# Retention: scores of two heads in turn, rotation and norm two steps ahead of the products that read them

## The chip, the cores and the metric

One core of a Trainium2 chip runs the whole kernel as one program. The metric is the device time of one execution in microseconds (us), the median of several runs.

## What is computed

The reference is a decoder of two layers over 1024 positions of width 1024. In each layer four mixers (softmax attention with forget gates, a gated linear recurrence, RWKV-7 and retention) each take 256 of the width, then come an output projection, cross attention and an MLP, each with norms around it. The change touches retention alone, with four heads of 64 and chunks of 128 positions:

```
qh = rotary(q); kh = rotary(k) / 8                    # per head, 64 wide
inner = einsum('bhcnd,bhcmd->bhcnm', qc, kc) * dmat   # scores in a chunk, decay mask
intra = einsum('bhcnm,bhcme->bhcne', inner, vc)
kv    = einsum('bhcmd,bhcme->bhcde', kc * zeta, vc)
R_next = R * chunk_decay + kv                         # state, chunk after chunk
cross = einsum('bhcnd,cbhde->bhcne', qc * xi, R)
o = head_rms_norm(intra + cross, w)                   # o * rsqrt(mean(o*o) + eps) * w, per head
return o * silu(g)
```

## The kernel before

One generator writes each branch of the mixer stage: the dense projections, RWKV in four quarters, the recurrence, the forget-gate attention (called fox), the keys and values of the memory, and retention (`ret`, from L943). A generator stops at each `yield`; one step of it is what stands between two of them. The function `weave` in `run`'s layer goes round: one step of each RWKV chain, one step of retention, then three or four pieces of `fill`, which are the dense products, fox and, at the end, the first products of the output projection. Retention begins with the last RWKV quarter. That quarter has 16 rounds, so 16 retention steps; after it `weave` runs retention alone with the fill, two of its steps and four fill pieces a round. The program is then built by a planner that orders each engine's queue by the written order and by when it expects operands and buffers to be ready, so that work written later can stand earlier in a queue. On the chip each queue runs in the order that it has.

A tile of retention is 128 positions, eight tiles a layer. Before the change it goes through four steps:

- `rotate` (L962): two loads on SP's queue (L964, L965), four VectorE instructions of the rotation (L970 to L974), the decayed keys (L976), the gate (L977 on ScalarE, L978), then four TensorE transposes into one PSUM bank (L981) and its two readers, a copy on ScalarE (L983) and a product on VectorE (L985).
- `retain`, first step: for each head of a pair two score products of 64 rows into one bank (L996), then the mask on VectorE (L997).
- `retain`, second step: the output products (L1001, L1004), the state products (L1010), the state update on VectorE (L1014), two readers of the output on ScalarE (L1016, L1017).
- `finish` (L1020): sum of squares (L1026), the power on GpSimd (L255, L256 in `rstd`), two multiplies on VectorE (L1028, L1029), two transposes into one bank (L1032), each followed by its scaled copy on ScalarE (L1033), and after every fourth tile two stores.

The loop (L1041) writes, in each pass, the rotation of tile tt, both steps of tile tt-1 and the finish of tile tt-2. All PSUM banks of retention, and those of the RWKV chain, are of the tag "r", which has two; a bank is waited for as a whole. The SBUF tiles of retention, RWKV and fox's weights are of one tag of 32 buffers (`q`, L487). A matmul on these float32 operands shows in the trace as two instructions.

Of the kernel before, what the change touches and what calls it, by code (L numbers as in the profile page):

```python
# [11 lines left out]
ALU = mybir.AluOpType  # L12
AX = mybir.AxisListType
# [9 lines left out]
EPS = 1e-6  # L23
GN_EPS = 64e-5
NT = S // 128
# [61 lines left out]
class Kern:  # L87
# [855 lines left out]
    def ret(self, l, tmq, tmv, mixd):  # L943
        nc = self.nc
        V, A, P, T = nc.vector, nc.scalar, nc.gpsimd, nc.tensor
        H = lambda shape=(128, 512), name="re": self.q(shape, name)
        tab = [H((128, 4, 2, 2, 32), name="rot") for _ in range(2)]
        for i in range(2):
            self.dma2(tab[i].rearrange("p a b c d -> p (a b c d)"), self.I["rot"][:, 512 * i:512 * i + 512])
        dm = H((128, 4, 128), name="rdm")  # L950
        self.dma2(dm.rearrange("p h n -> p (h n)"), self.I["retc"][:, 0:512])
        rc = H((128, 512), name="rec")
        self.dma2(rc[:, 0:256], self.I["retc"][:, 512:768])
        xi, Rb = (rc[:, 256 * i:256 * i + 256].rearrange("p (a n) -> p a n", a=2) for i in range(2))
        rz = self.small([128, 6], "rtz", 1)
        self.dma2(rz, self.I["retc"][:, 768:774])
        zeta, dec = rz[:, 0:4], rz[:, 4:6]
        V.memset(Rb, 0.0)
        hd = lambda ap: ap.rearrange("p (h d) -> p h d", h=4)
        out = {}  # L960

        def rotate(tt):  # L962
            x, vg, xc, xs = H(), H(), H(), H()
            self.dma2(x, tmq[tt])  # L964
            self.dma2(vg, tmv[tt])  # L965
            g = vg[:, 256:512]
            q8 = lambda ap: ap.rearrange("p (q h d) -> p q h d", q=2, h=8)
            cb = tab[tt // 4][:, tt % 4, :, 0, :].unsqueeze(2).to_broadcast([128, 2, 8, 32])
            sb = tab[tt // 4][:, tt % 4, :, 1, :].unsqueeze(2).to_broadcast([128, 2, 8, 32])
            V.tensor_tensor(q8(xc), q8(x), cb, ALU.mult)  # L970
            V.tensor_tensor(q8(xs), q8(x), sb, ALU.mult)
            g4 = lambda ap: ap.rearrange("p (g e d) -> p g e d", g=8, e=2)
            V.tensor_tensor(g4(x)[:, :, 0], g4(xc)[:, :, 0], g4(xs)[:, :, 1], ALU.subtract)
            V.tensor_tensor(g4(x)[:, :, 1], g4(xs)[:, :, 0], g4(xc)[:, :, 1], ALU.add)  # L974
            kz, sg = xc[:, 0:256], xc[:, 256:512]
            V.tensor_tensor(hd(kz), hd(x[:, 256:512]), zeta.unsqueeze(2).to_broadcast([128, 4, 64]), ALU.mult)  # L976
            A.activation(sg, g, AF.Tanh, scale=0.5)  # L977
            V.scalar_tensor_tensor(sg, sg, 1.0, g, ALU.add, ALU.mult)  # L978
            pt = self.psum("r", (128, 4, 128))
            for j in range(4):  # L980
                T.transpose(pt[:, j], x[:, 128 * j:128 * j + 128], self.ident)  # L981
            qk = H((128, 4, 128))
            A.copy(qk, pt)  # L983
            qx = xs[:, 0:256].rearrange("p (a n) -> p a n", a=2)
            V.tensor_tensor(qx, pt[:, 0:2], xi, ALU.mult)  # L985
            return x, vg, xc, xs, qk

        def retain(tt, x, vg, xc, xs, qk):
            v, kz = vg[:, 0:256], xc[:, 0:256]
            qx = xs[:, 0:256].rearrange("p (a n) -> p a n", a=2)  # L990
            inn = x.rearrange("p (a n) -> p a n", a=4)
            for h in range(2):
                pi = self.psum("r", (128, 2, 128))
                rs = slice(64 * h, 64 * h + 64)
                for ct in range(2):
                    T.matmul(pi[:, ct], qk[rs, 2 + ct], qk[rs, ct], start=True, stop=True)  # L996
                V.tensor_tensor(inn[:, h:4:2], pi, dm[:, h:4:2], ALU.mult)  # L997
            yield
            po = self.psum("r", (128, 256))
            for ct in range(2):  # L1000
                T.matmul(po[:, 128 * ct:128 * ct + 128], qx[:, ct], Rb[:, ct], start=True, stop=False)  # L1001
                for h in range(2):
                    c0 = 128 * ct + 64 * h
                    T.matmul(po[:, c0:c0 + 64], inn[:, 2 * ct + h], v[:, c0:c0 + 64], start=False, stop=h == 1)  # L1004
            if tt < NT - 1:
                pk = self.psum("r", (128, 2, 64))
                for ct in range(2):
                    for h in range(2):
                        c0 = 128 * ct + 64 * h
                        T.matmul(pk[64 * h:64 * h + 64, ct], kz[:, c0:c0 + 64], v[:, c0:c0 + 64], start=True, stop=True)  # L1010
                for ct in range(2):
                    for h in range(2):
                        rs = slice(64 * h, 64 * h + 64)
                        V.scalar_tensor_tensor(Rb[rs, ct, rs], Rb[rs, ct, rs], dec[rs, ct:ct + 1], pk[rs, ct],  # L1014
                                               ALU.mult, ALU.add)
            A.copy(xs[:, 256:512], po)  # L1016
            A.activation(xs[:, 0:256], po, AF.Square, scale=0.125)  # L1017
            yield

        def finish(tt, x, vg, xc, xs, qk):  # L1020
            if tt % 4 == 0:
                out[0] = [H((128, 512), name="ost") for _ in range(2)]
            ost = out[0]
            y, sg = xs[:, 256:512], xc[:, 256:512]
            ss = self.small([128, 4], "ress", 2)
            V.tensor_reduce(ss, hd(xs[:, 0:256]), AX.X, ALU.add)  # L1026
            r = self.rstd(ss, EPS, 4, "t")
            V.tensor_tensor(hd(y), hd(y), r.unsqueeze(2).to_broadcast([128, 4, 64]), ALU.mult)  # L1028
            V.tensor_tensor(y, y, sg, ALU.mult)  # L1029
            py = self.psum("r", (128, 2, 128))  # L1030
            for ct in range(2):
                T.transpose(py[:, ct], y[:, 128 * ct:128 * ct + 128], self.ident)  # L1032
                A.activation(ost[ct][:, (tt % 4) * 128:(tt % 4) * 128 + 128], py[:, ct], AF.Copy,  # L1033
                             scale=self.half(l, "ret_w", ct))
            if tt % 4 == 3:
                t0 = 512 * (tt // 4)
                for ct in range(2):
                    self.dma2(mixd[3][ct][:, t0:t0 + 512], ost[ct])

        st = {}  # L1040
        for tt in range(NT + 2):  # L1041
            if tt < NT:
                st[tt] = rotate(tt)
                yield
            if 0 <= tt - 1 < NT:
                yield from retain(tt - 1, *st[tt - 1])
            if tt >= 2:
                finish(tt - 2, *st.pop(tt - 2))
                yield


    def fox_gates(self, l, vfd, cd):
# [731 lines left out]
    def layer(self, l, hT, vfirst, first, pj):  # L1784
# [71 lines left out]

        tm = [0, 0]
        retg = ret()
        kv = [self.dram([128, 4, 256], "kd") for _ in range(2)], [self.dram([128, D], "vd") for _ in range(2)]
        x = self.xd[3 * l:3 * l + 4]  # L1860
# [160 lines left out]
```

## Time and profile before

| | |
|---|---|
| median of 3 runs | 3272.2 us (3271.38 to 3275.03) |
| the profiled execution | 3271.57 us, its span 3269.8 us |
| TensorE (PE) busy | 3116.0 us, 95% of the span |
| VectorE (DVE) | 2098.6 us, 64% |
| ScalarE (ACT) | 1307.2 us, 40% |
| GpSimd (POOL) | 804.6 us, 25% |
| mean granted TensorE clock | 0.978 of full speed |
| retention, layer 0 and layer 1 | from about 455 to 612 us and 2090 to 2242 us |

Matmuls are pipelined and their ends are modelled, so that the busy time of PE is not its rate: how far apart two instructions start tells more. A wait is shown with what released it. The clock is given as a part of full speed.

### The profile page before, as it was taken

Reading aid. Unit: us, or ns where it says so; the run is one execution under the profiler, and the core shown is the slowest. Engines: PE = TensorE matmul, PEld = TensorE weight load, DVE = VectorE, ACT = ScalarE, POOL = GpSimd, SP = SyncE. Lnnn points to the kernel's source line nnn. Section 1 sums busy time; section 2 is a strip of 40 time slices with the busy share of each in tenths; the row PEclk is TensorE's granted clock in tenths of the full one; section 3 lists DMA queues with packets and bytes.
Section 4 is the critical chain, followed back from the end, with each engine's and each line's share of the span. In section 5 each row is a group of like instructions: output and inputs, shape, how many; then the busy total and the mean of one; then the engine's idle time right before and its main releaser. Section 6 shows DMA issues by size and latency. Waiting matters only on the chain. (4 is left out here: it accounts for less than half of the span.)

```text
span 3269.8 us, 47116 instructions
## 1 busy us (share of the span) xinstructions
PE 3116.0 (95%) x17888; PEld 2526.2 (77%) x17888; DVE 2098.6 (64%) x3424; ACT 1307.2 (40%) x2396; POOL 804.6 (25%) x654
## 2 busy tenths in 40 slices
PE   8999999999998999899999999999999889999998
PEld 6777777878876888788777677778788768878886
DVE  4566567364457766888835765673644666668896
ACT  5345444343433222533433454443444432235332
POOL 1000121010014786333000001210100148853330
PEclk9999999999998999999999999999999999999999
DMA  5322363252333445544433234632523334455433
GB/s 176 103 85 91 112 201 110 75 189 73 110 110 107 157 152 183 176 164 138 140 131 111 97 88 116 201 94 97 168 78 97 116 114 152 154 176 196 156 132 125
DMA packets 220995, 429.31 MB, mean 131 GB/s; under 512 B 51136, under 2 KB 98368, under 8 KB 220768
## 3 DMA queue, kind: packets, MB, share of 16 engines
q1 hardware_dynamic: 214112, 409.32, 37.7%
q0 software_dynamic: 6656, 16.98, 2.1%
q8 instruction: 141, 2.31, 0.3%
q14 instruction: 86, 0.70, 0.1%
HBM read 294.51 MB, written 131.69 MB: 130 GB/s over the span
## 5 line engine op out<-in xcount | busy, mean ns | idle before, releaser
L212 PE MATMUL p<-hT,wl 128*128 128x512 f32 x1536 | 605.0, 395 | 17.2 <-DVE wl L198 17.0
L210 PE MATMUL p<-hT,wh 128*128 128x512 f32 x1536 | 615.7, 401 | 4.7 <-ACT mc L1526 2.5
L211 PE MATMUL p<-hT,wh 128*128 128x512 f32 x1536 | 605.1, 394 | 0.0
L198 DVE TENSOR_TENSOR wl<-wraw,wh 128x1024 fp32r<-128x1024 f32 (+1 forms) x230 | 281.2, 1223 | 346.6 <-ACT wh L197 345.9
L197 ACT CAST wh<-wraw 128x1024 fp32r<-128x1024 f32 (+1 forms) x230 | 240.0, 1044 | 487.7 <-POOL wraw L1472 182.4
L246 PE MATMUL p<-bo,ao 128*128 128x512 f32 x912 | 358.0, 393 | 15.7 <-DVE mb L1544 15.7
L248 PE MATMUL p<-bo,ao 128*128 128x512 f32 x912 | 357.2, 392 | 3.9 <-DVE bo L198 3.9
L247 PE MATMUL p<-bo,ao 128*128 128x512 f32 x912 | 357.4, 392 | 0.0
L212 PEld LDWEIGHTS p<-hT,wl 128*128 128x128 f32 x1536 | 291.8, 190 | 84.1 <-DVE wl L198 22.3
L210 PEld LDWEIGHTS p<-hT,wh 128*128 128x128 f32 x1536 | 292.1, 190 | 79.1 <-issue 13.2
L211 PEld LDWEIGHTS p<-hT,wh 128*128 128x128 f32 x1536 | 292.2, 190 | 57.5 <-issue 0.7
L246 PEld LDWEIGHTS p<-bo,ao 128*128 128x128 f32 x912 | 172.7, 189 | 52.6 <-DVE mb L1544 16.6
L246 PE MATMUL p<-wh,mt 128*128 128x512 f32 x512 | 204.6, 400 | 2.6 <-ACT wh L197 1.5
L248 PEld LDWEIGHTS p<-bo,ao 128*128 128x128 f32 x912 | 172.7, 189 | 40.8 <-DVE bo L198 4.7
L256 POOL TENSOR_TENSOR rs<-ssq,neghalf 128x1 f32<-128x1 f32 x48 | 26.1, 543 | 719.9 <-DVE ssq L303 533.1
L248 PE MATMUL p<-wl,mt 128*128 128x512 f32 x512 | 201.8, 395 | 0.6 <-DVE wl L198 0.5
L247 PE MATMUL p<-wh,mt 128*128 128x512 f32 x512 | 201.6, 394 | 0.0
L247 PEld LDWEIGHTS p<-bo,ao 128*128 128x128 f32 x912 | 172.6, 189 | 35.7
L198 DVE TENSOR_TENSOR ao<-araw,ao 128x1024 fp32r<-128x1024 f32 x106 | 173.2, 1634 | 14.1 <-ACT ao L197 14.0
L198 DVE TENSOR_TENSOR bo<-braw,bo 128x1024 fp32r<-128x1024 f32 x92 | 146.8, 1600 | 44.7 <-ACT bo L197 44.7
L197 ACT CAST bo<-braw 128x1024 fp32r<-128x1024 f32 x92 | 96.6, 1052 | 186.1 <-PE p L247 124.7
L197 ACT CAST ao<-araw 128x1024 fp32r<-128x1024 f32 x106 | 111.5, 1052 | 107.5 <-DMA araw<-hd 91.3
(393 smaller groups left out, 6303.8 us busy)
## 6 DMA issues: line engine op xcount, KB each, us to landing
araw<-hd SPq DMA_DIRECT2D x106, 512.0 KB, 4.0
x<-x SPq DMA_DIRECT2D x80, 512.0 KB, 3.5
wraw<-in_mlp_w SPq DMA_DIRECT2D x68, 512.0 KB, 3.5
braw<-in_mlp_w SPq DMA_DIRECT2D x64, 512.0 KB, 4.7
wraw<-in_w_fm SPq DMA_DIRECT2D x32, 512.0 KB, 3.8
pj<-spl SPq DMA_DIRECT2D x64, 256.0 KB, 2.1
hd<-mb SPq DMA_DIRECT2D x64, 256.0 KB, 2.5
hd<-mc SPq DMA_DIRECT2D x64, 256.0 KB, 2.0
```

What stands on the lines that cost most here:

```text
L197: self.nc.scalar.copy(h, src)
L198: self.nc.vector.tensor_tensor(lo, src, h, ALU.subtract)
L210: mm(ps, wh, xl, start=first, stop=False)
L211: mm(ps, wh, xh, start=False, stop=False)
L212: mm(ps, wl, xh, start=False, stop=last)
L246: mm(ps, xl, wh, start=first, stop=False)
L247: mm(ps, xh, wh, start=False, stop=False)
L248: mm(ps, xh, wl, start=False, stop=last)
L256: P.tensor_tensor(r, ss, self.neghalf[:, 0:k], ALU.pow)
```

## The change

In the new code `rotate` ends with the gate, and its transposes and their readers are a function of their own, `turned`. The scores are a function `scores`, which takes both banks first and issues the products of the two heads in turn, then both masks. The norm (`norm`) is split from `finish`, with the multiply by the gate moved ahead of the one that needs the power; `finish` issues both transposes and then both copies. The loop writes, for a tile: scores of tt and rotation of tt+1; then finish of tt-1 and the output and state of tt; then the transposes of tt+1; then the norm of tt. There are 37 steps a layer in place of 32.

```diff
+        def turned(x, vg, xc, xs):
             pt = self.psum("r", (128, 4, 128))
             for j in range(4):
                 T.transpose(pt[:, j], x[:, 128 * j:128 * j + 128], self.ident)
             qk = H((128, 4, 128))
             A.copy(qk, pt)
-            qx = xs[:, 0:256].rearrange("p (a n) -> p a n", a=2)
-            V.tensor_tensor(qx, pt[:, 0:2], xi, ALU.mult)
-            return x, vg, xc, xs, qk
+            V.tensor_tensor(xs[:, 0:256].rearrange("p (a n) -> p a n", a=2), pt[:, 0:2], xi, ALU.mult)
+            return qk
+
+        def scores(x, vg, xc, xs, qk):
+            inn = x.rearrange("p (a n) -> p a n", a=4)
+            pi = [self.psum("r", (128, 2, 128)) for _ in range(2)]
+            for ct in range(2):
+                for h in range(2):
+                    rs = slice(64 * h, 64 * h + 64)
+                    T.matmul(pi[h][:, ct], qk[rs, 2 + ct], qk[rs, ct], start=True, stop=True)
+            for h in range(2):
+                V.tensor_tensor(inn[:, h:4:2], pi[h], dm[:, h:4:2], ALU.mult)
...
         def retain(tt, x, vg, xc, xs, qk):
-            for h in range(2):
-                pi = self.psum("r", (128, 2, 128))
-                rs = slice(64 * h, 64 * h + 64)
-                for ct in range(2):
-                    T.matmul(pi[:, ct], qk[rs, 2 + ct], qk[rs, ct], start=True, stop=True)
-                V.tensor_tensor(inn[:, h:4:2], pi, dm[:, h:4:2], ALU.mult)
-            yield
...
-            yield
-
-        def finish(tt, x, vg, xc, xs, qk):
...
+        def norm(x, vg, xc, xs, qk):
             y, sg = xs[:, 256:512], xc[:, 256:512]
             ss = self.small([128, 4], "ress", 2)
             V.tensor_reduce(ss, hd(xs[:, 0:256]), AX.X, ALU.add)
             r = self.rstd(ss, EPS, 4, "t")
+            V.tensor_tensor(y, y, sg, ALU.mult)
             V.tensor_tensor(hd(y), hd(y), r.unsqueeze(2).to_broadcast([128, 4, 64]), ALU.mult)
-            V.tensor_tensor(y, y, sg, ALU.mult)
+
+        def finish(tt, x, vg, xc, xs, qk):
...
             for ct in range(2):
                 T.transpose(py[:, ct], y[:, 128 * ct:128 * ct + 128], self.ident)
+            for ct in range(2):
                 A.activation(ost[ct][:, (tt % 4) * 128:(tt % 4) * 128 + 128], py[:, ct], AF.Copy,
                              scale=self.half(l, "ret_w", ct))
...
-        st = {}
-        for tt in range(NT + 2):
-            if tt < NT:
-                st[tt] = rotate(tt)
-                yield
-            if 0 <= tt - 1 < NT:
-                yield from retain(tt - 1, *st[tt - 1])
-            if tt >= 2:
-                finish(tt - 2, *st.pop(tt - 2))
-                yield
+        st = {0: rotate(0)}
+        yield
+        yield
+        st[0].append(turned(*st[0]))
+        yield
+        for tt in range(NT):
+            scores(*st[tt])
+            if tt + 1 < NT:
+                st[tt + 1] = rotate(tt + 1)
+            yield
+            if tt:
+                finish(tt - 1, *st.pop(tt - 1))
+            retain(tt, *st[tt])
+            yield
+            if tt + 1 < NT:
+                st[tt + 1].append(turned(*st[tt + 1]))
+            yield
+            norm(*st[tt])
+            yield
+        yield
+        finish(NT - 1, *st.pop(NT - 1))
+        yield
```

## Rows read from the trace of the kernel before

**Rows 1.** Windows: busy us (instructions) of PE, PEld, DVE, ACT, POOL; clock, DMA, GB/s.

```profile
455.00:612.00 157.00, 147.30 (x1203) 118.07 (x1202) 110.08 (x253) 68.81 (x138) 25.18 (x37) 0.93 0.38 118
...
2090.00:2242.00 152.00, 142.27 (x1137) 115.06 (x1136) 108.77 (x261) 64.01 (x133) 21.18 (x31) 0.89 0.35 108
```

**Rows 2.** Waits of PE, whole run: total us, times, longest.

```profile
PE p L981 <- DVE re L974: 7.5, 4, 2.3
...
PE p L1032 <- DVE re L1029: 1.5, 2, 0.8
PE p L1032 <- ACT ost L1033: 1.3, 2, 0.9
```

**Rows 3.** Timeline of PE: start, us, line, tiles, count [idle before, releaser].

```profile
569.14 1.12 PE L981 MATMUL p<-ident,re 128*128 128x128 f32 x4 [2.08 <-DVE re L974]
...
2188.15 0.66 PE L981 MATMUL p<-ident,re 128*128 128x128 f32 x4 [1.32 <-DVE re L974]
...
2195.77 0.33 PE L1032 MATMUL p<-ident,re 128*128 128x128 f32 x1 [0.88 <-ACT ost L1033]
2197.83 1.12 PE L981 MATMUL p<-ident,re 128*128 128x128 f32 x4 [1.74 <-DVE re L974]
```

**Rows 4.** Windows of 10 us at the end of both retention stages.

```profile
560.00:570.00 10.00, 7.36 (x54) 6.00 (x53) 6.92 (x14) 5.28 (x11) 3.48 (x7) 0.94 1.06 274
570.00:580.00 10.00, 10.00 (x41) 7.89 (x40) 7.61 (x18) 3.22 (x7) 2.77 (x5) 0.50 0.34 89
580.00:590.00 10.00, 10.00 (x46) 7.70 (x44) 4.88 (x12) 4.30 (x10) 1.17 (x2) 0.88 0.26 86
...
2190.00:2200.00 10.00, 7.39 (x46) 5.27 (x44) 8.32 (x18) 4.56 (x11) 5.47 (x8) 0.85 0.70 218
2200.00:2210.00 10.00, 9.98 (x50) 9.30 (x49) 4.04 (x11) 2.35 (x6) 2.65 (x5) 0.50 0.08 23
2210.00:2220.00 10.00, 10.00 (x42) 9.17 (x42) 3.40 (x7) 2.73 (x6) 0.91 (x1) 0.50 0.43 132
```

**Rows 5.** Timeline of PE: products of 512 columns at either clock.

```profile
581.45 0.63 PE L246 MATMUL p<-wh,mt 128*128 128x512 f32 x1
581.88 0.63 PE L247 MATMUL p<-wh,mt 128*128 128x512 f32 x1
...
585.16 0.39 PE L247 MATMUL p<-wh,mt 128*128 128x512 f32 x1
585.39 0.39 PE L248 MATMUL p<-wl,mt 128*128 128x512 f32 x1
```

**Rows 6.** Timeline of PE: scores in a block of eight and of four.

```profile
503.75 0.77 PE L996 MATMUL p<-re 64*128 64x128 f32 x8
504.45 0.45 PE L1148 MATMUL p<-fo,fo 69*128 69x384 f32 x1
...
2190.44 0.71 PE L996 MATMUL p<-re 64*128 64x128 f32 x4
2191.08 0.49 PE L1001 MATMUL p<-rec,re 128*128 128x128 f32 x2
```

**Rows 7.** Groups by line: tiles, count | busy us, mean ns | idle before, releaser.

```profile
L970 DVE TENSOR_TENSOR re<-re,rot 128x512 f32<-128x512 f32 x16 | 10.9, 684 | 0.5 <-DMA re<-tq 0.5
...
L997 DVE TENSOR_TENSOR re<-p,rdm 128x256 f32<-128x256 f32 x32 | 13.3, 421 | 12.7 <-PE p L996 12.4
...
L1014 DVE SCALAR_TENSOR_TENSOR rec<-rec,rtz,p 64x64 f32<-64x64 f32 x56 | 15.6, 279 | 16.2 <-PE p L1010 15.2
...
L198 DVE TENSOR_TENSOR wl<-wraw,wh 128x1024 fp32r<-128x1024 f32 (+1 forms) x230 | 281.2, 1223 | 346.6 <-ACT wh L197 345.9
...
L256 POOL TENSOR_TENSOR rst<-ress,neghalf 128x4 f32<-128x4 f32 x16 | 16.7, 1045 | 1.2
...
L1033 ACT ACTIVATE ost<-p,pd 128x128 f32<-128x128 f32 x32 | 11.8, 369 | 25.6 <-PE p L1032 25.5
```

**Rows 8.** Waits of SP's queue, 450 to 620 us.

```profile
SPq L143 <- PE p L996: 15.7, 1, 15.7
```

More of the change, by code (lines that the diff above doesn't have):

```diff
@@ L978, in rotate @@
             V.scalar_tensor_tensor(sg, sg, 1.0, g, ALU.add, ALU.mult)
+            return [x, vg, xc, xs]
+        def turned(x, vg, xc, xs):
             pt = self.psum("r", (128, 4, 128))
@@ L1017, in retain @@
             A.activation(xs[:, 0:256], po, AF.Square, scale=0.125)
-            yield
-        def finish(tt, x, vg, xc, xs, qk):
-            if tt % 4 == 0:
-                out[0] = [H((128, 512), name="ost") for _ in range(2)]
-            ost = out[0]
+        def norm(x, vg, xc, xs, qk):
             y, sg = xs[:, 256:512], xc[:, 256:512]
@@ L1027, in finish @@
             r = self.rstd(ss, EPS, 4, "t")
+            V.tensor_tensor(y, y, sg, ALU.mult)
             V.tensor_tensor(hd(y), hd(y), r.unsqueeze(2).to_broadcast([128, 4, 64]), ALU.mult)
-            V.tensor_tensor(y, y, sg, ALU.mult)
+        def finish(tt, x, vg, xc, xs, qk):
+            if tt % 4 == 0:
+                out[0] = [H((128, 512), name="ost") for _ in range(2)]
+            ost, y = out[0], xs[:, 256:512]
             py = self.psum("r", (128, 2, 128))
```

## The prediction

> **What bounds the kernel now.** I read the stretches of the two retention stages first (one in each layer), then what TensorE waited for, then its timeline and granted clock around the longest of those waits, and last the engines that feed it.
>
> Retention runs from about 455 to 612 us in layer 0 and from 2090 to 2242 us in layer 1. In both, TensorE is the busiest engine (147.3 of 157 us and 142.3 of 152 us), VectorE follows at 70 and 72%, and ScalarE and GpSimd are far below [rows 1]. The matmuls of the other branches stand back to back between the retention's own, so a microsecond that TensorE spends there on a stall, on slow issue or at a low clock is a microsecond of the end time. The mean granted clock is 0.93 and 0.89 in these two stretches, lower than in most of the program [rows 1]: at 1.00 the same work would have taken up to 11 us and 17 us less.
>
> TensorE's own waits of the whole run hold three that belong to this code [rows 2]: the transposes of the rotated tile (L981) wait for the last rotation instruction (L974), 7.5 us in 4 waits; the transposes of the normed tile (L1032) wait for its last multiply (L1029), 1.5 us in 2; and the second of them waits until ScalarE has read the first one's half of the same bank (L1033), 1.3 us in 2. They sit in clusters [rows 3]: 0.88 us and 1.74 us directly one after the other at 2195.77 and 2197.83 in layer 1, 2.08 us at 569.14 in layer 0.
>
> Behind both late clusters the clock goes from 1.00 to 0.50 (2.4 to 1.2 GHz) and stays there for some 13 us and 24 us [rows 4]. While it is low, the same 512-column products start 0.43 us apart instead of 0.23 us [rows 5].
>
> **The change part by part**, in us of the end time, against the profiled execution's own 3271.57 us (span 3269.8 us and 1.8 us around it, which nothing here touches); the median of the runs, 3272.2 us, is 0.6 us above that.
>
> *Scores.* Each tile has four score products, which the trace shows as eight instructions. Of the 16 tiles of the two layers, 13 show two blocks of four, one for each head, with other work between; the next instruction starts 0.64 us after a block of four begins. Where the planner happened to put all eight together with the heads in turn, the block took 0.70 us [rows 6]; a second such block (2160.54) took 0.65, and one in the other order 1.07. So turning the heads saves 2 x 0.64 - 0.70 = 0.58 us a tile, 7.5 us for 13 tiles. The bounds are 0 (the planner splits them again) and about 10 (two of the 13 ran at the low clock, where a block took 1.15). I take 6.5: one tile in a layer may still be split while a bank is late.
>
> Two PSUM banks are needed at the same moment for this, and the tag has just two. In the kernel before, the second head took the bank of the tile's own transposes and had to wait for their two readers; this is why the blocks stand apart. In the new order six banks are drawn a tile (two for the scores, then one each for the normed transposes, the output, the state and the next transposes), so the scores get the banks of the state update and of the transposes, which were read two steps earlier.
>
> The Trainium skill speaks against this part: TensorEngine Tiling (Array Packing), Restrictions and Gotchas, says that products in different row tiles must write different banks and so raise the pressure on PSUM. By the trace both banks were free in three of 16 tiles in an order that made it harder. By the rule the pair would wait for the later bank, and the sum would lose this term (fourth rival below).
>
> *Rotation two steps ahead.* The rotation of tile tt+1 is written beside the scores of tile tt, and its transposes two steps later. The chain that the transposes wait for is four VectorE instructions, 2 x 0.69 + 2 x 0.42 = 2.2 us, behind the two mask multiplies of the scores, 0.84 us [rows 7]. What TensorE has in between now: the normed transposes (0.25), the output (1.4) and the state products (0.4), and one round of four fill pieces, which between 2188.15 and 2197.83 was about 1.6 us a round (9.7 us for two rounds, less 3.9 of retention's products and 2.6 of stall [rows 3]). That is 3.6 us over 3.0 us: covered, but thinly, and each split of another branch's tile (1.2 us [rows 7]) that stands between in VectorE's queue uncovers 0.6 us (3.0 + 1.2 - 3.6). Its two loads go out on SP beside the scores, one step before the old tile's buffers are dropped: 20 buffers of the shared tag are alive there against 21 before, and 16 instead of 20 in the other steps. SP once stood 15.7 us in front of such a load [rows 8], with weight loads queued behind it, so this should ease and not worsen.
>
> *Norm two steps ahead; both transposes before both copies.* The norm's chain is a reduce (0.42), GpSimd's power (1.05 [rows 7], with the small add before it 1.3) and now one multiply (0.42) in place of two: 2.2 us, under one block of scores (0.70) and a round of fill (1.6): just covered. The wait of the second transpose for ScalarE goes, since both are issued before the copies. No instruction is added on any engine; five more steps a layer only move ten fill pieces forward, and these are run in any case.
>
> Together the three waits are 10.3 us. All could go; I take 7, because the covers above are thin where VectorE is 83% busy (2190 to 2200 in rows 4). The bounds are 0 and 10.3.
>
> *Clock.* Low stretches: 0.6 + 5.0 + 1.2 us lost in layer 0 and 1.5 + 5.0 + 5.0 in layer 1 (each 10 us times what its clock lacks to 1.00), 18.3 in all [rows 4]; by the spacing 0.43 to 0.23 the loss is 0.47 of the time at half, 17 us. If the stalls in front of them go, TensorE has no reason to fall there. But it need not take all of a stall to make it fall, and a remainder is likely, so I take two thirds, 11. The bounds are 0 and 17; it is the largest and least certain term.
>
> *What comes in.* In the new bank order the state products (L1010) take the bank of the normed transposes and must wait for ScalarE's two copies, 0.37 each [rows 7]; the output products, 1.4 us, lie between. With other work as long as a split (1.2) ahead of them on ScalarE, 0.74 + 1.2 - 1.4 = 0.54 us shows. Between 0 and 16 x 0.54 = 8.6; I take 2.5, since ScalarE has the lighter queue.
>
> Sum: -6.5 - 7 - 11 + 2.5 = -22, so 3271.6 - 22 = 3249.6, forecast 3250.
>
> **Rivals.**
> *First, the clock falls anyway.* Waits of 1 to 2 us come back at L981 or L1004, since VectorE is 83% busy in the critical ten microseconds, and both low stretches stay. For it: the clock term hangs on two events. Against it: the single wait of 1.32 us at 2188.15 did not lower it, the block of four at 2190.44 behind it still took 0.64 [rows 3, 6]. Then -6.5 - 7 + 2.5 = -11: 3261.
> *Second, VectorE becomes the bound.* A tile costs it 2.2 (rotation), 0.84, 4 x 0.28 for the state [rows 7] and seven more of 0.42, 2.6 with their overlap: about 6.5 us, plus 2 or 3 us of the other branches, against some 6.5 us of TensorE. Then what TensorE saves on scores and stalls it waits elsewhere, and little is left, 3 or 4 us: 3268. For it: rows 4. Against it: over the stage VectorE is at 70%, and the planner pulls other matmuls forward.
> *Third, slower.* L1010's new wait for ScalarE's copies is not covered: the two copies, 0.74, and in two of three tiles 1.2 us of other work ahead of them, 1.5 us a tile with nothing over it, is 24 us for 16 tiles, less 6.5 + 7, with the clock as low as before: +10, 3282. It decides from 0.85 us a tile, (6.5 + 7) / 16. Against it: the output products lie in between, and ScalarE is only 42 to 44% busy [rows 1].
> *Fourth, the scores are not turned*: one of the two banks is still being read when the planner comes to them, so the first head's pair goes ahead alone, as in 13 of 16 tiles before. The blocks stay fours of 0.64 and the term is lost: -22 + 6.5 = -15.5: 3256. (It is what the rule cited above would bring.)
>
> **How the numbers follow.** Forecast 0.50 (own range 3236 to 3260), clock 0.20, VectorE 0.12, slower 0.10, scores not turned 0.08. A measurement of this kernel tells 0.2%, 6.5 us, from no change: faster is below 3265.7, slower above 3278.7. Forecast and fourth are faster, the clock rival mostly (0.17 of 0.20), 0.75 in all, of which I keep 0.74; VectorE's and the rest of the clock's are the same, 0.15; slower 0.11. The range 3234 to 3274 leaves out the third rival and the lowest part of the forecast, and contains the sum with any one term at its unfavourable end.
>
> **What would show it.** Right: L996 in blocks of eight of about 0.7 us; the waits L981 on L974 and L1032 on L1033 gone or under 2 us together; clock 1.00 through the last four tiles of both layers; the stage in layer 1 shorter by more than that in layer 0. Wrong: L996 still in fours; a new wait of L1010 on L1033, or of L981 on VectorE with the clock at 0.50 behind it; TensorE gaps spread over the stage with VectorE above 85%. A change of more than a few us outside 455 to 700 and 2090 to 2330 would mean that I looked in the wrong place.

## The result, and the profile after

The changed kernel takes 3254.06 us (median of five runs, 3247.4 to 3258.68) against 3271.38 us before (3270.01 to 3275.03): a ratio of 0.9941, 95% interval 0.9931 to 0.9952, or 17.3 us less. The profiled execution is the longest of its five, 3258.68 us with a span of 3256.9; the traces of the two kernels are 12.9 us apart.

The two retention stages, as in [rows 1]: busy time and instructions of TensorE, its weight loads, VectorE, ScalarE and GpSimd, then clock, DMA share and GB/s.

```profile
455.00:612.00 157.00, 146.55 (x1209) 116.82 (x1207) 112.98 (x266) 68.64 (x140) 25.84 (x37) 0.93 0.38 118
2090.00:2242.00 152.00, 146.22 (x1235) 116.56 (x1233) 110.55 (x267) 66.89 (x142) 20.81 (x31) 0.98 0.35 108
```

In layer 1 the granted clock rose from 0.89 to 0.98 and more instructions fit into the same 152 us. In layer 0 it stayed at 0.93. The ten-microsecond windows at the ends of both stages answer to [rows 4]:

```profile
560.00:570.00 10.00, 9.50 (x77) 8.27 (x76) 7.68 (x21) 3.80 (x10) 2.08 (x4) 1.00 0.62 211
570.00:580.00 10.00, 9.31 (x69) 7.44 (x68) 8.28 (x23) 6.49 (x13) 2.35 (x4) 1.00 0.20 52
580.00:590.00 10.00, 8.89 (x77) 7.78 (x76) 8.18 (x19) 5.72 (x15) 6.09 (x9) 1.00 0.68 192
2190.00:2200.00 10.00, 9.55 (x78) 8.24 (x77) 7.57 (x17) 6.50 (x14) 5.87 (x10) 1.00 0.69 196
2200.00:2210.00 10.00, 8.71 (x70) 7.67 (x70) 6.27 (x17) 5.12 (x11) 3.19 (x6) 1.00 0.90 236
2210.00:2220.00 10.00, 10.00 (x67) 8.24 (x67) 7.57 (x20) 4.01 (x11) 1.57 (x3) 0.83 0.07 27
```

Both long stretches at half clock are gone: 13.7 us near 570 and 23.9 us from 2197. In layer 1 one of 3.4 us is left there, and in layer 0 one of 3.4 from 595.6. Layer 0 lost its gain at another place. Behind a wait of the recurrence's solve (L771, code that the change doesn't touch; 4.45 us here, 3.9 before) the clock was low for 17.1 us where it had been for 6.8. The wait, then 470 to 490 before and now:

```profile
468.68 0.77 PE L771 MATMUL p<-Ds,Nq 32*32 32x32 f32 x64 [4.45 <-DVE Ds L766]
```

```profile
470.00:480.00 10.00, 10.00 (x178) 7.44 (x178) 6.05 (x12) 7.36 (x14) 0.00 (x0) 0.84 0.51 185
480.00:490.00 10.00, 10.00 (x69) 7.57 (x68) 9.39 (x24) 3.48 (x6) 0.00 (x0) 1.00 0.50 180
```

```profile
470.00:480.00 10.00, 10.00 (x155) 7.57 (x154) 4.00 (x7) 5.64 (x11) 0.00 (x0) 0.50 0.49 156
480.00:490.00 10.00, 10.00 (x53) 6.92 (x51) 6.43 (x14) 2.83 (x4) 0.00 (x0) 0.68 0.37 117
```

TensorE's waits of the whole run that answer to [rows 2] (waiting line, what released it; total us, times, longest):

```profile
PE p L246 <- DVE mt L198: 1.9, 1, 1.9
PE p L1041 <- DVE re L1033: 1.8, 3, 0.7
...
PE p L999 <- ACT re L988: 1.7, 2, 1.3
PE p L999 <- DVE rec L1022: 0.9, 1, 0.9
```

The transposes of the rotated tile (now L986) no longer wait, nor do those of the normed tile (L1041) for ScalarE's copies (L1043). 1.8 us of waits for the norm's last multiply (L1033) are left, and the scores (L999) have two new waits, 1.7 us for the copy of the transposed tile (L988) and 0.9 us for the state update (L1022). That is 10.3 us before and 4.4 after.

To see what the clock is worth I took, in every trace of this study, the time between the same two products of the 512-column projections, one near 2040 us and one near 2340 (2351 in the kernel before), and in it the time at half clock and TensorE's idle time:

```
layer 1, us           time   at half clock   idle
before                311.7      37.5        15.0
after                 300.0      10.2        12.4
```

The time fell by 11.7 us. 27.3 us less at half clock, at the 0.47 lost in each that the prediction took from [rows 5], is 12.8 us; idle time gives 2.6. The sum is over by 3.7 us. Some 1.5 of that is counted twice, since 3.3 us of the half-clock time before, and none after, was idle time too; the rest I did not follow up. The same taken in layer 0 (near 430 to near 700) is 271.8 against 270.1 us, with 20.5 us at half clock in both.

### The profile page after: what moved, and what is told of

Read it like the earlier page. It is cut to its first block, busy times and chain, and to the rows that moved or that the text cites. A ratio compares the mean times of both kernels' runs of the same rounds, so it can differ in the third digit from the quotient of the medians.

```text
span 3256.9 us, 47146 instructions
## 1 busy us (share of the span) xinstructions
PE 3108.7 (95%) x17888; PEld 2517.2 (77%) x17888; DVE 2100.9 (65%) x3424; ACT 1303.8 (40%) x2396; POOL 803.5 (25%) x654
## 5 line engine op out<-in xcount | busy, mean ns | idle before, releaser
L198 DVE TENSOR_TENSOR wl<-wraw,wh 128x1024 fp32r<-128x1024 f32 (+1 forms) x230 | 281.8, 1225 | 340.1 <-ACT wh L197 339.5
L246 PE MATMUL p<-bo,ao 128*128 128x512 f32 x912 | 357.8, 392 | 14.5 <-DVE mb L1567 14.5
L246 PEld LDWEIGHTS p<-bo,ao 128*128 128x128 f32 x912 | 172.5, 189 | 50.8 <-DVE mb L1567 15.3
L246 PE MATMUL p<-wh,mt 128*128 128x512 f32 x512 | 204.0, 398 | 3.7 <-DVE mt L198 1.9
L198 DVE TENSOR_TENSOR ao<-araw,ao 128x1024 fp32r<-128x1024 f32 x106 | 173.0, 1632 | 13.4 <-ACT ao L197 13.2
L198 DVE TENSOR_TENSOR bo<-braw,bo 128x1024 fp32r<-128x1024 f32 x92 | 146.6, 1597 | 43.2 <-ACT bo L197 43.2
```

The lines of the kernel that those rows point to most:

```text
L198: self.nc.vector.tensor_tensor(lo, src, h, ALU.subtract)
L246: mm(ps, xl, wh, start=first, stop=False)
```

## The experiments

Each is one edit, timed beside the kernel before on its own chip in the same rounds. Ratios are to that.

**Scores by head again.**

```
-            pi = [self.psum("r", (128, 2, 128)) for _ in range(2)]
-            for ct in range(2):
-                for h in range(2):
...
+            for h in range(2):
+                pi = self.psum("r", (128, 2, 128))
+                for ct in range(2):
```

> Edit: the changed kernel with its scores written one head after the other, as before the change. Theory (the planner that orders the queue puts a head's two products together whichever way they are written, so the turn in the source changes nothing that the engine sees): the time of the changed kernel, 3247 to 3259, middle 3253, and the score products of retention stand as after: some tiles as two fours of 0.64 us, the others as eights of 0.65 to 1.1. Rival (the turn is worth the 6.5 us of the prediction): about 3260, and every tile as two fours of 0.64.

Measured: 3258.3 us, ratio 0.9958 (0.9944 to 0.9972); the changed kernel's own interval overlaps this. The compiled queues of both are the same on all five engines apart from line numbers: the planner issues both products of head 0, then both of head 1, in whichever order they are written. The trace has the same blocks at the same tiles: eight tiles as two fours of 0.64 us, seven as one eight, one cut in three. The time alone would not tell the theory from the rival; the equal queues do. So turning the scores, as written, changed nothing, and this run is a second measurement of the change.

**Norm late.**

```
             if tt:
+                norm(*st[tt - 1])
                 finish(tt - 1, *st.pop(tt - 1))
...
-            norm(*st[tt])
```

> Edit: the changed kernel with the norm of a tile moved back into the step of the transposes that read it (L1041). Theory (the norm standing ahead is what took the waits of these transposes on VectorE's last multiplication of the norm away, and few of them cost the clock): waits of L1041 on L1033 come back, 3 to 6 us, and the time is 3256 to 3262, middle 3258. Rival (the norm's place does nothing, the rotation's does all): within 2 us of the changed kernel, 3252 to 3256, with at most 2 us of waits on L1033.

Measured: 3264.18 us, ratio 0.9978 (0.9968 to 0.9987), 5.9 us above the run by head on the same chip, whose interval just overlaps this one's. The waits on L1033 are 3.2 us, as the theory had it; the time is 2 us above its range, and the rival falls. The place ahead is worth some 6 us by this pair, 12 by the ratio of the first run of the change. TensorE's timeline (start, us, line, tiles, count, idle before and releaser) and windows:

```profile
2206.94 1.48 PE L999 MATMUL p<-re 64*128 64x128 f32 x8 [1.92 <-DVE rec L1022]
2210.70 1.12 PE L1224 MATMUL p<-ident,fot 128*128 128x128 f32 x4 [2.27 <-DVE fot L1219]
2211.47 0.78 PE L1196 MATMUL p<-fo,fo 128*128 128x512 f32 x1
```

```profile
2200.00:2210.00 10.00, 6.50 (x57) 5.86 (x56) 7.14 (x18) 4.18 (x10) 3.44 (x6) 0.87 0.85 183
2210.00:2220.00 10.00, 9.30 (x58) 7.33 (x58) 7.40 (x19) 5.37 (x12) 1.34 (x3) 0.79 0.35 107
2220.00:2230.00 10.00, 10.00 (x70) 8.37 (x70) 7.96 (x18) 4.44 (x10) 2.41 (x3) 1.00 0.00 1
```

The two waits are larger than any single one of layer 1 in [rows 3], and yet the half clock that begins behind the first of them lasts 6.8 us, not 23.9.

**Rotation late.**

```
             scores(*st[tt])
-            if tt + 1 < NT:
-                st[tt + 1] = rotate(tt + 1)
             yield
...
             if tt + 1 < NT:
+                st[tt + 1] = rotate(tt + 1)
                 st[tt + 1].append(turned(*st[tt + 1]))
```

> Edit: the changed kernel with the rotation of a tile moved back into the step of the transposes that read it (L986). Theory (the waits of these transposes on ScalarE and VectorE, 7.5 us before, bring the clock down for the last tiles of both layers, and the rotation ahead takes both away): the waits of L986 come back, 4 to 8 us, TensorE stands at half its clock for 15 us and more longer than in the changed kernel, and the time is 3263 to 3270, middle 3266. Rival (the waits have gone because retention starts at another place against the other work in the queue, not because of the rotation's place): 3252 to 3257, with no waits of L986.

Measured: 3277.41 us, ratio 1.0019 (1.0008 to 1.0029): 19 us above the run by head and slightly slower than the kernel before. The rival falls. The theory's direction holds and its sizes don't: the time lies above its 3263 to 3270, and the waits of L986 on the rotation are 11.3 us, more than expected.

```profile
2195.14 0.45 PE L1018 MATMUL p<-re,re 128*64 128x64 f32 x8 [2.92 <-ACT ost L1043]
2197.84 1.09 PE L986 MATMUL p<-ident,re 128*128 128x128 f32 x4 [2.25 <-DVE re L975]
2199.66 1.22 PE L999 MATMUL p<-re 64*128 64x128 f32 x4 [0.73 <-ACT re L988]
...
2202.76 5.33 PE L1210 MATMUL p<-fo,fpt 128*128 128x65 f32 x24
...
2211.53 6.24 PE L1210 MATMUL p<-fo,fpt 128*128 128x65 f32 x28
2217.52 0.77 PE L246 MATMUL p<-wh,mt 128*128 128x512 f32 x1
...
2222.69 0.48 PE L246 MATMUL p<-wh,mt 128*128 128x512 f32 x1
```

Three waits stand ahead of the sixth tile's scores (2199.66). Behind them come 52 product instructions of the attention branch with 65 columns, at 0.22 us each, and the clock is low from 2196.3 to 2220.2. In the changed kernel the same run of products, behind the same tile, has full clock, and the wait comes only behind it:

```profile
2193.86 0.60 PE L986 MATMUL p<-ident,re 128*128 128x128 f32 x4
...
2195.14 0.71 PE L999 MATMUL p<-re 64*128 64x128 f32 x4 [0.45 <-ACT re L988]
...
2196.91 3.74 PE L1211 MATMUL p<-fo,fpt 128*128 128x65 f32 x32
...
2208.78 1.17 PE L999 MATMUL p<-re 64*128 64x128 f32 x8 [1.29 <-ACT re L988]
2209.88 0.64 PE L246 MATMUL p<-wh,mt 128*128 128x512 f32 x1
```

The same product takes 0.117 us here (3.74 / 32).

**Scores held in turn.**

```
+            with self.tc.tile_critical():
                 for ct in range(2):
                     for h in range(2):
```

> Edit: the changed kernel with the four products of a pair's scores held together in their written order, so that the two heads really stand in turn in the queue. Theory (two fours of 0.64 us apart against eights of 0.65 to 0.73 us: 9 of 16 tiles gain some 0.6 us): 5 us less than the changed kernel, 3247 to 3251, and eights of 0.65 to 0.75 us in all 16 tiles. Rival (the first product now waits for the second head's bank too, and what the eights save is waited for): 3253 to 3262, with more waits ahead of the score products than the 2.6 us of the changed kernel.

Measured: 3327.77 us, ratio 1.0169 (1.0154 to 1.0185). Neither time is met. The rival's waits ahead of the scores do come, but not for the second bank: the four products stand in turn, and TensorE now waits ahead of them for things they don't read, loads of other branches among them:

```profile
PE p L1000 <- DMA fo<-in_foxq: 7.1, 1, 7.1
PE p L1000 <- DMA re<-tq: 5.5, 1, 5.5
PE p L1000 <- issue: 4.8, 2, 4.4
PE p L1000 <- DMA mx<-W: 3.7, 1, 3.7
```

Eight of the ten blocks at full clock take 0.81 us each, no less than an eight that stands by head without a wait (0.65 to 0.75). What a turn would save without this hold stays open; that adjacent heads save, the 0.65 against twice 0.64 shows.

**A later start.** The kernel before, with empty steps:

```
             if tt < NT:
                 st[tt] = rotate(tt)
                 yield
+                if tt == 0:
+                    yield
+                    yield
+                    yield
```

> Edit: the kernel before, with three empty steps behind its first rotation, so that the rest of retention stands three steps later against the work that is dealt out beside it. Theory (the gain comes from the rotation and the norm standing ahead of the products that read them, not from where retention starts): within 5 us of the kernel before, 3267 to 3276, with 5 us and more of waits of the transposes L985 (L981 before) on VectorE or ScalarE and a half-clock stretch of 10 us and more in both retention stages. Rival (the start alone decides which tiles lack other work): 3254 to 3262, and the waits gone.

Measured: 3287.84 us, ratio 1.0056 (1.0044 to 1.0068). The rival falls, and so does the theory's "within 5 us": a later start costs 18 us. Half clock holds for 47.8 us from 2191, and begins in this wait:

```profile
2193.64 1.09 PE L981 MATMUL p<-ident,re 128*128 128x128 f32 x4 [3.52 <-issue]
```

**Rotation late for some tiles.** The two halves of the edit "rotation late", split at the fifth and sixth tile:

```
-            if tt + 1 < NT:
+            if tt + 1 < 5:
                 st[tt + 1] = rotate(tt + 1)
...
             if tt + 1 < NT:
+                if tt + 1 >= 5:
+                    st[tt + 1] = rotate(tt + 1)
```

> Edit: the changed kernel with the rotation moved back into the step of the transposes that read it for the last three of the eight tiles of each layer alone. Theory (the waits fall where TensorE has no other work left, which is at the last tiles; what stands under the earlier ones hides them): most of the loss of moving all of them, 12 to 20 us above the changed kernel, 3267 to 3275, with the long half-clock stretches near 580 and 2207. Rival (every tile loses its part): 3/7 of that loss, 3262 to 3265.

> Edit: the other half of the one before: the rotation of the second to fifth tile of each layer stands in the step of its transposes, that of the last three stands ahead as in the changed kernel. Theory (the early tiles have other work beside them): within 4 us of the changed kernel, 3253 to 3260, no wait of L986 above 2 us and no half-clock stretch above 10 us behind 560 and 2190. Rival (every tile loses its part): 4/7 of the loss, 3265 to 3268.

Measured: late for the last three 3263.44 us (3250.0 to 3272.5), ratio 0.9977 (0.9963 to 0.999); late for the second to fifth 3276.92 us, ratio 1.003 (1.0018 to 1.0042). The theory has the order wrong: the early tiles cost more. The rival's time for the last three, 3262 to 3265, is met, but the late head lies 9 us above its 3268 and costs as much as all tiles together (1.003 against 1.0019). Why the early tiles do this was not followed further than this: the late head has its waits again ahead of the sixth tile's scores (2203.64), some of them not for the rotation at all.

```profile
2191.26 0.63 PE L986 MATMUL p<-ident,re 128*128 128x128 f32 x4 [1.37 <-DVE re L975]
...
2198.72 0.44 PE L1197 MATMUL p<-fo,fo 128*128 128x384 f32 x1 [1.76 <-ACT fpt L1201]
2201.67 1.12 PE L986 MATMUL p<-ident,re 128*128 128x128 f32 x4 [0.89 <-ACT re L1025]
2203.64 1.58 PE L999 MATMUL p<-re 64*128 64x128 f32 x8 [0.85 <-DVE rec L1022]
```

```profile
2190.00:2200.00 10.00, 6.78 (x41) 5.21 (x41) 5.67 (x16) 4.56 (x9) 4.50 (x8) 0.96 0.70 174
2200.00:2210.00 10.00, 8.26 (x45) 7.39 (x44) 7.75 (x19) 3.47 (x9) 2.36 (x5) 0.50 0.67 211
2210.00:2220.00 10.00, 10.00 (x54) 9.76 (x53) 2.87 (x9) 2.89 (x7) 0.00 (x0) 0.50 0.00 0
```

The profiled execution of the late tail (3250.0 us, the fastest of its twelve) has small waits there and no fall at the end of either stage:

```profile
2185.26 0.71 PE L999 MATMUL p<-re 64*128 64x128 f32 x4 [0.68 <-ACT re L988]
2192.50 0.45 PE L1018 MATMUL p<-re,re 128*64 128x64 f32 x8 [0.89 <-ACT ost L1043]
```

Over its twelve runs the time goes with the mean granted clock, 0.985 and 0.987 at 3250 and 3251 us, 0.977 to 0.980 at 3272: by that the clock falls more in some executions than in others, and the one trace doesn't stand for the median.

**Rotation ahead, alone**, in the kernel before, first with two steps more at the start, then with none. It stands one step ahead of its transposes here, where the change has it two ahead:

```
         def rotate(tt):
...
+            return [x, vg, xc, xs]
+
+        def turned(x, vg, xc, xs):
             pt = self.psum("r", (128, 4, 128))
...
             if tt < NT:
-                st[tt] = rotate(tt)
+                st[tt].append(turned(*st[tt]))
...
                 finish(tt - 2, *st.pop(tt - 2))
+            if tt + 1 < NT:
+                st[tt + 1] = rotate(tt + 1)
```

> Edit: the kernel before, with its rotation cut from the transposes and put one step ahead of them; scores, norm and last transposes stay as they were. Theory (the rotation's place is the larger part of the gain): the waits of the first transposes on rotation and their half-clock stretches go, 3256 to 3264; waits of L1032's transposes on the norm stay, up to 3 us. Rival (the rotation ahead brings nothing without the norm ahead and the later start): 3268 to 3276.

> Edit: the kernel before, with its rotation cut from the transposes and put one step ahead of them, and no step more at the start, so that the first scores stand in the same step as before (in the earlier run of this edit they stood two steps later). Theory (its loss there came from the later start, which costs some 6 us a step as the run with three empty steps shows; the rotation's place by itself is worth the larger part of the gain): 3256 to 3265. Rival (the rotation alone brings nothing): 3270 to 3280.

Measured: 3279.48 us, ratio 1.003 (1.0018 to 1.0041), and 3268.7 us, ratio 0.9996 (0.9987 to 1.0006). Both theories fail, and the times lie 3 us above and 1 us below the ranges of their rivals. Most of the first one's loss was its later start, and the rotation alone, one step ahead, brings nothing. In the second one its transposes (L984) still wait 8.9 us, 3.23 of them ahead of the sixth tile's scores, and layer 1's 23.9 us at half clock stay:

```profile
2198.72 1.12 PE L984 MATMUL p<-ident,re 128*128 128x128 f32 x4 [3.23 <-DVE re L974]
```

So this is no test of a rotation two steps ahead, which leaves no wait of that kind in the changed kernel.

**Filler in the waits.** The kernel before, with

```
             pt = self.psum("r", (128, 4, 128))
+            for j in range(6 if tt >= 5 else 0):
+                T.transpose(pt[:, j % 4], self.ident, self.ident)
```

> Edit: the kernel before, with six extra transposes of the identity matrix written into the same bank ahead of the real transposes of the last three tiles of each layer (36 products of about 0.27 us, 9.8 us if none lies in idle time); they wait for nothing but the bank, so they stand where TensorE waited for the rotation. Theory (TensorE's idle time at the last tiles is what brings the half clock behind it): the long half-clock stretches near 580 and 2207 (13.7 and 23.9 us before) shrink to under 8 us each, which gives back some 14 us; the time is 3258 to 3268 although work was added. Rival (the clock falls there because of what the other engines and the transfers do at that place): the stretches stay, and the time is 3273 to 3282.

Measured: 3276.51 us, ratio 1.002 (1.0011 to 1.0029). The rival's time, but not its condition: the idle time was moved and not filled, and the filler itself waited 6.5 us for its bank. A wait of the normed transposes now stands ahead of the same products (scores at 2202.4), and the clock is low for 27.3 us behind it.

```profile
2200.84 0.30 PE L1034 MATMUL p<-ident,re 128*128 128x128 f32 x1 [1.73 <-DVE re L1031]
```

So it doesn't separate idle time from what else goes on there; that question stays open.

**An earlier start**, the changed kernel without one and without both of the empty steps behind its first rotation:

```
         st = {0: rotate(0)}
-        yield
         yield
         st[0].append(turned(*st[0]))
```

> Edit: the changed kernel without one of the two empty steps behind its first rotation, so that retention starts one step earlier, in the step of the kernel before. Theory (an earlier start leaves more other work beside the last tiles): 0 to 6 us under the changed kernel, 3247 to 3254. Rival (the empty steps keep the first tile clear of the recurrence solve that runs there): 3258 to 3266.

> Edit: the changed kernel without both empty steps, retention two steps earlier. Theory: 0 to 10 us under the changed kernel, 3244 to 3254, the half clock behind 2200 at 4 us or less. Rival (the first tiles fall among the solves and bring their waits): 3260 to 3272.

Measured: 3260.37 us, ratio 0.997 (0.9959 to 0.9982), and 3254.39 us, ratio 0.9954 (0.9937 to 0.9971). Layer 1 has no long fall in either, as the theory of the second said, but nothing is gained against the change. The second comes out at the upper end of its theory's range. The first misses its own and lies in its rival's; the wait at the solve did not grow, though (1.7 us at L771, 4.45 in the change). It has 20.5 us at half clock at the end of layer 0. No version here beats the changed kernel beyond its interval.

All traces together, one execution each, in order of layer 1's time between the two products named above; the last column has the waits from about 2184 us on that stand ahead of the long run of 65-column products or, in the late tail, also inside it:

```
kernel                    time   at half   waits there
after, start 1 earlier    297.8     3.4     0.57
after, late tail          299.0     6.8     0.37, 0.68, 0.89
by head                   299.2     6.8     0.44
after, start 2 earlier    299.5     6.8     0.20
after                     300.0    10.2     0.45
norm late                 302.5    13.7     0.21
before                    311.7    37.5     1.32, 0.88, 1.74
before, filler            312.1    37.5     1.73, 0.54
rotation alone            314.1    30.7     0.92, 0.54, 1.70, 3.23
late head                 314.2    34.1     1.37, 0.20, 1.76, 0.89, 0.85
rotation late             315.7    30.7     1.34, 2.92, 2.25, 0.73
rotation alone, 2 later   318.0    37.5     0.23, 1.75, 0.59, 0.49
before, 3 later           325.7    58.0     0.42, 3.52, 0.46, 0.54
```

(In after, by head, norm late and the start two earlier the larger waits, 1.3 to 2.3 us, stand behind that run. The kernel with the scores held is left out: it waits all over the stage.) There are two groups and nothing between them: 298 to 303 us with 3 to 14 us at half clock, and 312 to 326 with 31 to 58.

Layer 0 bears this out in one pair. The changed kernel and the one that starts one step earlier have the same run, 32 and then 20 of these instructions, behind the same scores, with a wait for the state update ahead of it that differs by half a microsecond (after, then start 1 earlier):

```profile
583.86 1.07 PE L999 MATMUL p<-re 64*128 64x128 f32 x8 [0.91 <-DVE rec L1022]
585.21 3.74 PE L1211 MATMUL p<-fo,fpt 128*128 128x65 f32 x32
```

```profile
579.16 1.58 PE L999 MATMUL p<-re 64*128 64x128 f32 x8 [1.37 <-DVE rec L1022]
581.28 7.04 PE L1210 MATMUL p<-fo,fpt 128*128 128x65 f32 x32
```

The first keeps full clock over the run, the second is at half for 20.5 us. Over both layers of these thirteen kernels, the nine falls of 20.5 us and more (to 47.8) hold all 52 of these instructions, and the clock came back within the run in none of them. No other fall there holds more than two of them, and the others last 17.1 us at most (layer 0 of rotation late, with a wait of 7.74 us; 13.7 in the kernel before). So such a run isn't needed for a fall, but the longest ones all go over it.

## Why the prediction came out

**The time was right, and so was the largest term.** The forecast was 3250 against 3254.06. The clock was sized at 11 us; in the two traces layer 1 alone returns some 11 to 13, by the 0.47. The mechanism (waits at the end of the stage, then half clock) is what goes with the two groups of the table. But the prediction had each wait count for its size, and the clock follow "if the stalls in front of them go". By the runs their place counts as well: the norm-late kernel's 1.92 and 2.27 us behind the run of 65-column products went with 6.8 us at half clock; 1.73 us ahead of it (filler) went with 27.3. Size counts there too: the first group of the table has no single wait above 0.9 us ahead of that run, and each kernel of the second has one of 1.7 or more. Shown is the coincidence in thirteen traces; why the clock stays low over the one and not over the other, these runs do not settle.

**In layer 0 the term came to nothing in the trace.** Its late fall went as forecast, but an early one, behind a wait in another branch, grew by 10.3 us. That one differs between runs of one queue (17.1 us after, 10.2 by head), and by head layer 0 takes 264.9 us, 5.2 less than in the trace after. The prediction's sign "the stage in layer 1 shorter by more than that in layer 0" holds: 11.7 against 1.7 us.

**The waits were sized well**: 7 us of 10.3 forecast, 5.9 measured by name. L981's wait went fully, L1033's copies' too, L1029's did not (1.5 before, 1.8 on L1033 after), and two waits of the scores came, 2.6 us together. The cover that the prediction reckoned for the rotation (3.6 us over 3.0) holds in the trace: the last rotation instruction (L975) ends 0.4 us and more ahead of every tile's transposes.

**The scores were mis-sized: 6.5 forecast, about 1.7 measured.** "So turning the heads saves 2 x 0.64 - 0.70 = 0.58 us a tile" failed at its first step, since the planner undoes the order in the source. The prediction misread its own row as well: in the compiled queue of the kernel before, too, both products of head 0 stand ahead of both of head 1 in every tile, so the block that took 0.70 didn't have its heads in turn. What changed is only that seven tiles have both heads standing together (0.65 to 1.10 us each), against three before: 26 blocks at 17.4 us against 29 at 21.2, of which 1.7 us is order and the rest blocks no longer at half clock. This is the fourth rival in effect, which had a chance of 0.08 and a time of 3256, nearer to the result than the forecast. It happened in nine of sixteen tiles.

The Trainium skill's rule on PSUM pressure (TensorEngine Tiling (Array Packing), Restrictions and Gotchas), which the prediction set against this term, says that row tiles write to different banks, and the prediction made of it a wait for the later one. No run here shows whether the banks made the planner split the pairs.

**L1018's new wait did not come.** 2.5 us forecast, none in the trace: the copies (L1043) end 0.2 us and more ahead of the state products each time. In the rotation-late kernel it does come, 2.92 us once, so the price was there and the cover held.

**The other rivals.** VectorE is busier in layer 1's stage (110.6 of 152 us against 108.8, or 73%), below the 85% that the prediction named as a sign. "The clock falls anyway" is what six of the other kernels do in layer 1, but not the change. SP's queue, which was to ease, lost its 15.7 us on L996 and stands 18.0 us for the gate on ScalarE (L978; 11.4 before); no wait of TensorE follows from it in the trace.

**Errors that cancel.** The terms that were measured, -1.7 for the scores, -5.9 for the waits and about -13 for the clock, make -20.6, close to the forecast's -22. That is luck in part: 4.8 us of the scores' saving did not come, and neither did the 2.5 charged for L1018. The two traces differ by 12.9. Of the 7.7 between, 3.2 are other waits that grew (idle time of both stretches fell by 2.7, not 5.9; one is L246 on L198, 1.9 us, at the start of layer 0's output projection). The rest is the 3.7 of layer 1 above and small differences. That the medians differ by 17.3 owes something to the profiled execution being the longest of its five.

**Which part does it.** The rotation ahead is needed: 19 us are lost without it, and the norm ahead does not make up for that (1.0019). The norm ahead is worth 6 by its pair, and without it some of the gain stays (0.9978). The rotation by itself was tried one step ahead only, and gives 0.9996; two steps ahead by itself was not run. What goes with the gain is less the size of their waits than a queue in which nothing is late by much ahead of that run of 65-column products.

## What to carry to other kernels

Look up where a wait stands, and not its size alone: 2.3 us of waits ahead of a long stretch of narrow products go with 12 us here (filler, 312.1 against 300.0 us in the table), while 4.2 us of waits a little later go with 2.5 (norm late, 302.5). When a planner orders the queue, read the order from the trace before pricing an order written in the source. And test an edit to the staging with its neighbours in place, and at its full distance: taking the rotation back by two steps cost the changed kernel 19 us, and putting it one step ahead gave the kernel before nothing.

## What was not expected of the hardware

In the kernel before half clock held for 23.9 us, and TensorE waited only in the first 0.8 of them: it ran retention's products and 65-column ones at about 0.22 us each, then 512-column ones, and was back at full clock from about 2221:

```profile
2214.32 3.93 PE L1188 MATMUL p<-fo,fpt 128*128 128x65 f32 x18
...
2218.01 0.77 PE L246 MATMUL p<-wh,mt 128*128 128x512 f32 x1
...
2222.40 0.39 PE L248 MATMUL p<-wl,mt 128*128 128x512 f32 x1
```

And one compiled queue gave executions of 3250 to 3272 us on one chip (late tail), with the mean granted clock between 0.987 and 0.977.
